# Storing the first slab in one piece and loading the projections in halves, in a kernel bound by its transfers

## The chip, the core and the metric

The kernel runs on one core of a Trainium2 chip. The core has five engines with queues of their own (TensorE or PE, VectorE or DVE, ScalarE or ACT, GpSimd or POOL, SyncE or SP) and 16 DMA engines that move data between the off-chip memory (HBM) and the on-chip memory. The metric is the time of one execution on the device in microseconds (us), as the median of several. Time from the profile is counted from the span's start, which is the first instruction of the program.

## What is computed

```python
def reference(x, conditioning, gamma_proj, beta_proj):
    gamma = conditioning @ gamma_proj
    beta = conditioning @ beta_proj
    return (x * (1 + gamma[:, None, :]) + beta[:, None, :]).astype(np.float32)
```

All is float32. `x` is 32 x 512 x 256 (batch, sequence, channels), 16.8 MB; the output has the same size. `conditioning` is 32 x 64, each projection 64 x 256. Every element of `x` is read once, multiplied by one plus its gamma, has its beta added, and is written once.

## The kernel before

The batch is cut into four slabs of eight batch entries. A slab is a tile of 128 partitions with 32 rows of 256 channels each: 32 KB a partition, 4 MB in all. All four slabs stay in on-chip memory at once (`xs0` to `xs3`), the results overwrite the inputs there, and no buffer is used again.

**Loads.** SP issues all loads of `x` in order at the start (L60): slab 0 in four parts of eight rows (8 KB a partition), then slabs 1, 2 and 3 whole (32 KB a partition). ACT issues three small loads at the start: the conditioning (L49) and then the two projections into the halves of one tile `gbproj` (L51, L52), each 64 rows of 1 KB.

**Gamma and beta.** A matrix product with a widened identity (L73) turns the conditioning round and repeats each batch entry 16 times, so that each of 128 partitions has its entry's conditioning; DVE copies that to `cond_T` (L75). For each slab one matrix product on PE (L80) with `gbproj` gives gamma and beta for the slab's 128 partitions in PSUM (`gb_p`), and ACT copies both to on-chip memory, with 1 added to gamma (L83, L86), as `gb_s`. The first L80 waits for both projections.

**The main loop.** For each slab there are two groups of 16 rows. DVE does the first 11 rows of a group with two instructions (L101: gamma plus one times x; L104: plus beta) and POOL the other five (L103, L105). POOL's two L103 of a slab come before its two L105 in the order as built; DVE keeps the written order. So slab 0's first eight rows need nothing from POOL.

**Stores.** ACT issues the stores (L109), each as soon as the group that holds its last row is done. `STORES` says which rows go together: slab 0 in parts that end at rows 2, 8 and 32, so 2, 6 and 24 rows, or 2, 6 and 24 KB a partition; slabs 1 to 3 whole. The first two parts are issued after the first group, the third after the second.

**What sets the order.** Each engine runs its own instructions in order. Loads of `x` go through SP's DMA queue (q1 in the profile); the small loads and all stores go through ACT's (q10). Both are served by the same 16 DMA engines. A transfer with 128 partitions is cut into 128 packets, one per partition row, eight per DMA engine, and each DMA engine also writes one 4-byte completion per transfer. Completions go round eight semaphores, so a transfer's issue can wait for an earlier transfer that used the same one. SP ends the program only after all transfers have landed (the waits on L136).

Of the kernel before, what the change touches and what calls it, by code (L numbers as in the profile page):

```python
# [2 lines left out]

# [5 lines left out]


@with_exitstack
def kernel(
    ctx: ExitStack,
    tc: tile.TileContext,
    x: bass.AP,
    conditioning: bass.AP,
    gamma_proj: bass.AP,
    beta_proj: bass.AP,
    out: bass.AP,  # L20
):
    nc = tc.nc
    f32 = mybir.dt.float32
    ALU = mybir.AluOpType

    batch, seq, dim = x.shape
    cond_dim = conditioning.shape[1]
    P = 128
    SLABS = 4
    BS = batch // SLABS  # L30
    REP = P // BS
    ROWS = BS * seq // P
    assert SLABS * BS == batch and REP * BS == P and ROWS * REP == seq

    x_v = x.flatten_outer_dims().rearrange("(s p r) d -> s p r d", s=SLABS, p=P)
    o_v = out.flatten_outer_dims().rearrange("(s p r) d -> s p r d", s=SLABS, p=P)

    LOADS = {0: [8, 8, 8, 8]}
    STORES = {0: (2, 8, 32), 1: (32,), 2: (32,), 3: (32,)}
    GROUP = 16  # L40
    ON_DVE = 11

    consts = ctx.enter_context(tc.tile_pool(name="consts", bufs=1))
    xpool = ctx.enter_context(tc.tile_pool(name="xpool", bufs=1))
    psum = ctx.enter_context(tc.tile_pool(name="psum", bufs=1, space=bass.MemoryType.PSUM))


    cond_s = consts.tile([batch, cond_dim], f32)
    nc.scalar.dma_start(out=cond_s, in_=conditioning)  # L49
    gbproj = consts.tile([cond_dim, 2 * dim], f32)  # L50
    nc.scalar.dma_start(out=gbproj[:, :dim], in_=gamma_proj)  # L51
    nc.scalar.dma_start(out=gbproj[:, dim:], in_=beta_proj)  # L52

    slabs = []
    for s in range(SLABS):
        xs = xpool.tile([P, ROWS, dim], f32, name=f"xs{s}")
        slabs.append(xs)
        r = 0
        for n in LOADS.get(s, [ROWS]):
            nc.sync.dma_start(out=xs[:, r : r + n, :], in_=x_v[s, :, r : r + n, :])  # L60
            r += n
        assert r == ROWS


    ident = consts.tile([batch, batch], f32)
    make_identity(nc, ident)
    rident = consts.tile([batch, batch * REP], f32)
    nc.vector.tensor_copy(  # L68
        out=rident.rearrange("p (b g) -> p b g", g=REP),
        in_=ident.to_broadcast([batch, batch, REP]),  # L70
    )
    cond_T_p = psum.tile([cond_dim, batch * REP], f32)
    nc.tensor.matmul(cond_T_p, lhsT=cond_s, rhs=rident, start=True, stop=True)  # L73
    cond_T = consts.tile([cond_dim, batch * REP], f32)
    nc.vector.tensor_copy(out=cond_T, in_=cond_T_p)  # L75

    gb_p, gb_s = [], []
    for s in range(SLABS):
        p_t = psum.tile([P, 2 * dim], f32, name=f"gb_p{s}")
        nc.tensor.matmul(p_t, lhsT=cond_T[:, s * P : (s + 1) * P], rhs=gbproj,  # L80
                         start=True, stop=True)
        s_t = consts.tile([P, 2 * dim], f32, name=f"gb_s{s}")
        nc.scalar.activation(out=s_t[:, :dim], in_=p_t[:, :dim],  # L83
                             func=mybir.ActivationFunctionType.Identity,
                             bias=1.0, scale=1.0)
        nc.scalar.copy(out=s_t[:, dim:], in_=p_t[:, dim:])  # L86
        gb_p.append(p_t)
        gb_s.append(s_t)

    def rows(t, n):  # L90
        return bass.AP(tensor=t.tensor, offset=t.offset, ap=[t.ap[0], [0, n], t.ap[1]])

    for s in range(SLABS):
        xs = slabs[s]
        g_p, b_p = gb_p[s][:, :dim], gb_p[s][:, dim:]
        g_s, b_s = gb_s[s][:, :dim], gb_s[s][:, dim:]
        for r0 in range(0, ROWS, GROUP):
            v = xs[:, r0 : r0 + ON_DVE, :]
            w = xs[:, r0 + ON_DVE : r0 + GROUP, :]
            nv, nw = ON_DVE, GROUP - ON_DVE  # L100
            nc.vector.scalar_tensor_tensor(out=v, in0=rows(g_p, nv), scalar=1.0, in1=v,  # L101
                                           op0=ALU.add, op1=ALU.mult)
            nc.gpsimd.tensor_tensor(out=w, in0=w, in1=rows(g_s, nw), op=ALU.mult)  # L103
            nc.vector.tensor_add(out=v, in0=v, in1=rows(b_p, nv))  # L104
            nc.gpsimd.tensor_tensor(out=w, in0=w, in1=rows(b_s, nw), op=ALU.add)  # L105

            for e0, e1 in zip((0,) + STORES[s], STORES[s]):
                if r0 < e1 <= r0 + GROUP:
                    nc.scalar.dma_start(out=o_v[s, :, e0:e1, :], in_=xs[:, e0:e1, :])  # L109
        assert STORES[s][-1] == ROWS  # L110


# [1 line left out]
_INS = ['x', 'conditioning', 'gamma_proj', 'beta_proj']  # L114
_OUTS = [((32, 512, 256), 'float32')]


# [23 lines left out]
```

## Time and profile before

| | |
|---|---|
| median of 3 runs | 84.33 us (84.33 to 84.34) |
| the profiled execution's own time | 84.33 us |
| its span, first to last instruction | 82.6 us |
| bytes moved | 33.69 MB, mean 408 GB/s |
| packets | 2080 |
| DVE busy | 49.9 us (60% of the span) |
| POOL busy | 46.3 us (56%) |
| PE busy | 9.1 us (11%) |
| ACT busy | 3.9 us (5%) |
| first instruction of the main loop on DVE | 12.10 us |
| last instruction on DVE, end | 61.18 us |

The profile page gives, for each engine, the busy time and a strip of 40 slices (about 2 us each) with the busy share in tenths; the strip named DMA is the mean busy share of the 16 DMA engines. The chain is followed back from the last instruction to what released each step. A group of instructions has the source line, the engine, the operation, and the mean duration of one. The list of DMA issues gives the size of each transfer and its time "to landing", from issue to the completion of its last packet. Asked for a window, the trace gives the packets that start in it for each queue, their bytes, and the time they took as a share of 16 engines over the window. Packets of different lines can be compared in this way: a window that holds one size of packet on one queue gives the duration of a single packet.

### The profile page before, as it was taken

To read this page: it belongs to the slowest core of one execution; us is meant where nothing else is said; L and a number is where in the kernel's file an instruction comes from. 1 tells how busy PE (TensorE), PEld (TensorE's weight loads), DVE (VectorE), ACT (ScalarE), POOL (GpSimd) and SP (SyncE) were. 2 spreads that over 40 slices of the span, in tenths; PEclk is the share of its full clock that TensorE was granted. 3 is DMA by queue.
4 is the path that set the end of the run, shared out by engine and by line. 5 is a ranking of instruction groups with operands and counts; after the bars stand their busy time and mean duration, and the time that the engine had idled before them with its cause. 6 is when DMAs were issued, how large, how long until landed. Compare 5 with 4: busy or idle time off the path is not lost.

```text
span 82.6 us, 154 instructions
## 1 busy us (share of the span) xinstructions
PE 9.1 (11%) x10; PEld 2.8 (3%) x10; DVE 49.9 (60%) x18; ACT 3.9 (5%) x9; POOL 46.3 (56%) x22
## 2 busy tenths in 40 slices
PE   0090499900000000000000000000000000000000
PEld 0010243100000000000000000000000000000000
DVE  2002019999999999999999999999960000000000
ACT  0600033330000000000000000000000000000000
POOL 2000029999999999999999999999000000000000
DMA  3899999799899796979997999998998998999890
GB/s 48 322 422 380 421 425 591 333 429 508 351 458 508 303 539 284 605 318 460 445 445 302 453 476 405 508 397 365 508 460 349 460 508 349 413 508 413 349 508 0
DMA packets 2080, 33.69 MB, mean 408 GB/s; under 512 B 288, under 2 KB 416, under 8 KB 672
## 3 DMA queue, kind: packets, MB, share of 16 engines
q1 hardware_dynamic: 1008, 16.78, 48.7%
q10 hardware_dynamic: 1072, 16.92, 47.8%
HBM read 16.92 MB, written 16.78 MB: 408 GB/s over the span
## 4 chain that ended last, share of the span: by engine, by line
DVE 48%; issue 12%; DMA 9%; PE 2%; ACTq 1%; ACT 1%
DVE xs L101 30%; DVE xs L104 19%; DMA gbproj<-in_beta_proj_dram 9%; PE gb_p L80 2%; ACTq L51 1%; ACTq L49 0%; ACT gb_s L83 0%; ACT gb_s L86 0%
## 5 line engine op out<-in xcount | busy, mean ns | idle before, releaser
L103 POOL TENSOR_TENSOR xs<-xs,gb_s 128x1280 f32<-128x1280 f32 x8 | 23.0, 2898 | 11.0 <-ACT gb_s L83 10.8
L101 DVE SCALAR_TENSOR_TENSOR xs<-gb_p,xs 128x2816 f32<-128x2816 f32 x8 | 24.7, 3085 | 5.3 <-ACT gb_s L86 5.3
L104 DVE TENSOR_TENSOR xs<-xs,gb_p 128x2816 f32<-128x2816 f32 x8 | 24.7, 3088 | 0.3
L105 POOL TENSOR_TENSOR xs<-xs,gb_s 128x1280 f32<-128x1280 f32 x8 | 23.0, 2893 | 0.0
L80 PE MATMUL gb_p<-gbproj,cond_T 64*128 64x512 f32 x8 | 7.2, 1074 | 3.3 <-DMA gbproj<-in_beta_proj_dram 3.3
L75 DVE COPY cond_T<-cond_T_p 64x512 f32<-64x512 f32 x1 | 0.7, 682 | 4.5 <-PE cond_T_p L73 4.5
L80 PEld LDWEIGHTS gb_p<-gbproj,cond_T 64*128 64x128 f32 x8 | 2.5, 326 | 8.1 <-issue 8.1
L73 PE MATMUL cond_T_p<-rident,cond_s 32*64 32x512 f32 x2 | 1.9, 1068 | 4.1 <-DMA cond_s<-in_conditioning_dram 4.1
L83 ACT ACTIVATE gb_s<-gb_p 128x256 f32<-128x256 f32 x4 | 1.5, 385 | 11.0 <-PE gb_p L80 11.0
L86 ACT COPY gb_s<-gb_p 128x256 f32<-128x256 f32 x4 | 1.5, 368 | 0.0
L83 ACT ACT_TABLE_LOAD x1 | 1.3, 1283 | 2.4 <-issue 2.4
L68 DVE COPY rident<-ident 32x512 f32<-32x512 f32 x1 | 0.4, 414 | 1.2 <-POOL ident masks.py:199 1.2
L73 PEld LDWEIGHTS cond_T_p<-rident,cond_s 32*64 32x64 f32 x2 | 0.3, 198 | 4.1 <-issue 4.1
masks.py:197 POOL MEMSET ident<- 32x32 f32 x1 | 0.1, 116 | 0.3 <-POOLq L125 0.3
masks.py:199 POOL TENSOR_SCALAR_AFFINE_SELECT ident<-ident 32x32 f32<-32x32 f32 x1 | 0.2, 205 | 0.1
L125 POOL MEMSET const-float32-0.0<- 128x1 f32 x1 | 0.1, 104 | 0.2 <-issue 0.2
L125 POOL MEMSET const-uint8-127<- 128x1 uint8 x1 | 0.1, 108 | 0.0
L125 POOL MEMSET const-bfloat16-1.0<- 128x1 bf16 x1 | 0.1, 106 | 0.0
L125 POOL MEMSET const-float32-1.0<- 128x1 f32 x1 | 0.1, 103 | 0.0
## 6 DMA issues: line engine op xcount, KB each, us to landing
xs<-in_x_dram SPq DMA_DIRECT2D x3, 4096.0 KB, 26.2
out_dram<-xs ACTq DMA_DIRECT2D x3, 4096.0 KB, 23.1
xs<-in_x_dram SPq DMA_DIRECT2D x4, 1024.0 KB, 8.5
out_dram<-xs ACTq DMA_DIRECT2D x1, 3072.0 KB, 28.2
out_dram<-xs ACTq DMA_DIRECT2D x1, 768.0 KB, 25.1
out_dram<-xs ACTq DMA_DIRECT2D x1, 256.0 KB, 14.0
gbproj<-in_gamma_proj_dram ACTq DMA_DIRECT2D x1, 64.0 KB, 6.4
gbproj<-in_beta_proj_dram ACTq DMA_DIRECT2D x1, 64.0 KB, 7.5
```

Of the source, the lines that this page charges most:

```text
L51: nc.scalar.dma_start(out=gbproj[:, :dim], in_=gamma_proj)
L68: nc.vector.tensor_copy(out=rident.rearrange("p (b g) -> p b g", g=REP), in_=ident.to_broadcast([batch, batch, REP]),)
L73: nc.tensor.matmul(cond_T_p, lhsT=cond_s, rhs=rident, start=True, stop=True)
L75: nc.vector.tensor_copy(out=cond_T, in_=cond_T_p)
L80: nc.tensor.matmul(p_t, lhsT=cond_T[:, s * P : (s + 1) * P], rhs=gbproj, start=True, stop=True)
L83: nc.scalar.activation(out=s_t[:, :dim], in_=p_t[:, :dim], func=mybir.ActivationFunctionType.Identity, bias=1.0, scale=1.0)
L86: nc.scalar.copy(out=s_t[:, dim:], in_=p_t[:, dim:])
L101: nc.vector.scalar_tensor_tensor(out=v, in0=rows(g_p, nv), scalar=1.0, in1=v, op0=ALU.add, op1=ALU.mult)
L103: nc.gpsimd.tensor_tensor(out=w, in0=w, in1=rows(g_s, nw), op=ALU.mult)
L104: nc.vector.tensor_add(out=v, in0=v, in1=rows(b_p, nv))
L105: nc.gpsimd.tensor_tensor(out=w, in0=w, in1=rows(b_s, nw), op=ALU.add)
L125: nc = _bacc.Bacc("TRN2", target_bir_lowering=False, num_devices=1)
```

## The change

Two edits. The store of slab 0 goes out whole, like those of the other slabs. Each projection is loaded by two DMAs of 32 rows each, in place of one of 64. The sizes and the order of the loads of `x`, the computation and its order on PE, DVE and POOL stay as they are. ACT issues five small loads in place of three and four stores in place of six; the numbers of lines after L52 go up by one.

```diff
-    STORES = {0: (2, 8, 32), 1: (32,), 2: (32,), 3: (32,)}
+    STORES = {0: (32,), 1: (32,), 2: (32,), 3: (32,)}
...
-    nc.scalar.dma_start(out=gbproj[:, :dim], in_=gamma_proj)
-    nc.scalar.dma_start(out=gbproj[:, dim:], in_=beta_proj)
+    for half, proj in ((gbproj[:, :dim], gamma_proj), (gbproj[:, dim:], beta_proj)):
+        for c0 in range(0, cond_dim, 32):
+            nc.scalar.dma_start(out=half[c0 : c0 + 32, :], in_=proj[c0 : c0 + 32, :])
```

## The prediction

> **What bounds the kernel now.** I read the page's row of DMA by slices first, then the chain of work, then the waits of the DMA queue's engine (SP), then the time to landing of single DMAs by narrow windows.
>
> From the page:
> ```profile
> span 82.6 us, 154 instructions
> DMA  3899999799899796979997999998998998999890
> ...
> DVE 48%; issue 12%; DMA 9%; PE 2%; ACTq 1%; ACT 1%
> ...
> xs<-in_x_dram SPq DMA_DIRECT2D x3, 4096.0 KB, 26.2
> out_dram<-xs ACTq DMA_DIRECT2D x3, 4096.0 KB, 23.1
> ```
> From the waits of SP:
> ```profile
> SPq L136 <- DMA out_dram<-xs: 47.7, 4, 18.8
> ```
> The DMA row is at eight or nine tenths in nearly every slice from 2 to 80 us. The chain names DVE, but it follows instructions back from DVE's last one, which the timeline ends at 61.2 us (58.09 + 3.09). The other 21 us are the stores still draining: SP's final waits are on the output. So the end is set by how long the 16 DMA engines need for all bytes, provided that they never run dry.
>
> The price of a transfer, from windows of the DMA view (first window 22.35 to 30.3 us, second 33 to 42, third 52.5 to 80; q1 carries the x loads, q10 the stores):
> ```profile
> q1 hardware_dynamic: 114, 3.21, 93.6%
> q10 hardware_dynamic: 115, 0.24, 7.6%
> ```
> ```profile
> DMA packets 230, 3.96 MB, mean 440 GB/s; under 512 B 15, under 2 KB 15, under 8 KB 131
> ...
> q1 hardware_dynamic: 114, 3.24, 83.5%
> q10 hardware_dynamic: 116, 0.71, 18.9%
> ```
> ```profile
> q10 hardware_dynamic: 394, 11.86, 99.9%
> ```
> The columns are packets, MB and share of 16 engines. Two readings. First, packets go one for one: 114 against 115, though a load packet is 32 KB and a store packet here 2 KB. An engine with work in both queues gives them **turns**, whatever the size. Second, the price: 0.076 x 7.95 us x 16 engines / 115 = 0.084 us for a 2 KB packet; 0.189 x 9 x 16 / 116 = 0.234 us for 6 KB; 0.999 x 27.5 x 16 / 362 (394 less 32 completions) = 1.213 us for 32 KB. The window 44.5 to 51.8 gives 0.912 us for 24 KB in the same way. A slab has 128 packets, 8 per engine: 9.70 us.
>
> So today the slab-0 store in thin rows hardly slows the loads, and pays for it in its own landing: the 256 KB part is issued at 18.35 and takes 14.0 us. The last x load lands at 46.3 (8.73 + 37.6), 2.5 us before DVE wants that slab:
> ```profile
> 45.84 3.09 DVE L104 TENSOR_TENSOR xs<-xs,gb_p 128x2816 f32<-128x2816 f32 x1
> ...
> 48.85 3.08 DVE L101 SCALAR_TENSOR_TENSOR xs<-gb_p,xs 128x2816 f32<-128x2816 f32 x1
> ```
>
> **The projections in halves (L51, L52).** ACT issues four DMAs of some 0.5 us in place of two (0.51 and 0.61). The same 128 rows of 1 KB move, but each engine gets two more completions, so two more turns behind 8 KB x packets. Gamma lands at 1.17 + 6.4 = 7.6, beta at 1.72 + 7.5 = 9.2: 1.6 us for beta's five turns (four rows and a completion), 0.32 each, so the last half lands 0.65 us later, at 9.86. L80, which waits for it (9.34), L83, L86 and the whole DVE chain (12.10) move with it. In the built order the eight completion semaphores shift round: the fourth slab-0 load now waits for cond_s (landed at 4.0), the slab-1 load for the first slab-0 part (5.6), slab 2 for gamma's first half and slab 3 for beta's first half. SP then issues slab 1 some 3 us later than at 2.86, but its packets' turn comes at 12.7, behind 4 MB, so that costs nothing. With fewer x issues ahead of them the halves may also land earlier. Bounds: 0.65 us sooner to 1.3 us later; I take +0.65. None of it reaches the end while the engines have x to load. In the engines' own time, the ten projection turns stand in a stretch where 8 KB packets run somewhat slow (about 0.2 us per engine altogether); two turns more are an estimate of +0.04, bounds -0.2 and +0.2.
>
> **The slab-0 store whole (L109).** Removed are two ACT issues and, per engine, 8 packets each of 2, 6 and 24 KB: 8 x (0.084 + 0.234 + 0.912) = 9.84 us. Added are 8 of 32 KB: 9.70. That is **-0.14 us**. Completions are equal (nine DMAs on this queue before and after).
>
> Two short stalls stand in the trace where one slab-0 part hands over to the next while loads run. In the windows 31.4 to 32.05 and 43 to 43.6, the sixteen load packets take:
> ```profile
> q1 hardware_dynamic: 16, 0.52, 194.8%
> ```
> ```profile
> q1 hardware_dynamic: 16, 0.52, 247.9%
> ```
> That is 1.948 x 0.65 = 1.27 us and 2.479 x 0.6 = 1.49 us a packet, 0.05 and 0.28 over 1.213. Two hand-overs become one (slab 0 to slab 1). If it costs as the first row, 0.28 goes; if the second row belongs to the last load packet of all, that recurs and only 0.05 goes. Bounds: -0.33, and +0.23 if the one left costs both rows' worse figure twice. I take the middle of the two readings, -0.17.
>
> **What moves: the loads of slabs 2 and 3.** The store is now issued after the whole slab, at 24.52 + 0.65 = 25.2. Today no q10 packet starts between 18.35 and 22.3, so a store finds its first turn 4.0 us after issue: 29.2, on the packet grid about 29.7. From 22.4 to there six of slab 2's eight packets have gone. The other two take turns with stores: with the completion's turn and 0.9 us to landing, slab 2 is there at 36.6, due at 36.60 + 0.65 = 37.25: no wait. Slab 3's eight then each pay a 32 KB store: 8 x 2.43, less one turn that slab 0's completion takes; they run to 55.2 and land at **56.1**. DVE wants them at 48.85 + 0.65 = 49.5: a new stall of 6.6 us. The slab takes 12.33 us (48.85 to 61.18), so it is done at 68.5, and its store is issued at 68.6, not 61.26.
>
> Does that show at the end? At 55.2 each engine has served 11 store packets (25.5 us / 2.43) and has 13 left of slabs 0 to 2: 13 x 1.213 = 15.8, to 70.9. Slab 3's packets must be ready by then. The first load shows issue to first packet on a free queue: 0.74 to about 1.75, 1.0 us. So 69.6, with **1.3 us to spare**. The DVE stall is hidden by the backlog, and if that cover goes, every microsecond counts in full.
>
> The Trainium skill ("DMA: Bandwidth & Descriptors", "Queues, rings and completion order") says that an engine drains a whole packet of typically 9 to 17 descriptors from one ring before it switches. This trace disagrees, with its 114 against 115. By that rule slab 0's eight would go in one piece, slab 3 would land near 52, and nothing could run dry; the sum would be the same.
>
> **Sum.** 84.33 - 0.14 - 0.17 + 0.04 = 84.06; I say 84.05. The profiled execution took 84.33 (span 82.6, 1.7 around it), the median of the three runs, so no correction is needed.
>
> **Rivals.** About 0.2% (0.17 us) is what a measurement here can tell from no change: below 84.16 is faster, over 84.50 slower.
> (A) As summed: the engines never run dry, 83.85 to 84.3. For it: the full DMA row. Chance 0.60, of it 0.42 faster, 0.18 same.
> (B) The engines run dry before the last store, which ends slower. The 4.0 us of the first store may be a latency of a loaded queue rather than its place behind packets already taken in; gamma, too, is issued at 1.17 and has its first packet only at 5.27. Then slab 3's packets come at 68.6 + 4.0 = 72.6 against 70.9: +1.7, in all 85.8. It decides from a latency of 2.3 us. Loads that come one packet later give up 1.2 us of the same margin, earlier projections likewise, so 84.5 to 85.8. Against it: 1.0 us on the free queue. Chance 0.28, of it 0.03 same.
> (C) Reads and writes of 32 KB in turn run slower than either alone. They alternate for 25.5 us, so each per cent is 0.26 us; at 2%, 84.6. Against it: 440 GB/s in the mixed window 33 to 42, no less than elsewhere. Chance 0.12, of it 0.03 same.
> Faster 0.42, same 0.24, slower 0.34. The range goes from A with both stalls gone (83.8) nearly to B's full price (85.6).
>
> **What would show it.** x landing to its maximum near 47 us (slab 3 issued near 9, landing at 56), a DVE wait of about 6.6 us before the seventh L101, DVE's end at 68.5, the last store landing about 13 us after its issue, the DMA row full to the end. A dip in the DMA row near slice 34 or 35 (70 to 72 us) is B. If slab 3 lands before 52, the turns are not as I read them; if more than 58, the engines will run dry and the prediction is wrong.

## The result, and the profile after

The changed kernel takes 84.69 us (median of six runs, 84.56 to 85.03) against 84.36 for the kernel before in the same comparison: a ratio of 1.0047, 95% interval 1.0025 to 1.0068. It is slower by about 0.33 us. Here and below, a median is of all runs, and a ratio is of the means of those runs that lie within 1.5% of the same kernel's fastest. The profiled execution took 84.56 (span 82.8), 0.23 more than the one of before.

The page of the changed kernel, the lines that answer to those shown of before, with the packet line and the queues:
```profile
span 82.8 us, 155 instructions
...
DMA  2799999899979989699799969969997996998890
...
DMA packets 1824, 33.69 MB, mean 407 GB/s; under 512 B 288, under 2 KB 416, under 8 KB 416
...
q1 hardware_dynamic: 1008, 16.78, 48.8%
q10 hardware_dynamic: 816, 16.92, 47.5%
...
DMA 67%; DVE 15%; ACTq 2%; issue 0%; DVEq 0%
...
out_dram<-xs ACTq DMA_DIRECT2D x4, 4096.0 KB, 22.6
xs<-in_x_dram SPq DMA_DIRECT2D x3, 4096.0 KB, 31.5
```
The DMA row is still full to the end. The chain now runs through transfers (67% DMA, 59% the loads of `x` alone), since DVE waits for the loads. The two queues of the kernel before:
```profile
q1 hardware_dynamic: 1008, 16.78, 48.7%
q10 hardware_dynamic: 1072, 16.92, 47.8%
```
Put the queues' shares on their spans: q10 took 0.475 x 82.8 = 39.3 us of 16 engines, before 0.478 x 82.6 = 39.5; q1 took 0.488 x 82.8 = 40.4, before 0.487 x 82.6 = 40.2. The stores got slightly cheaper and the unchanged loads dearer.

The timeline of DVE shows the new waits, before slab 2 (1.1 us) and before slab 3 (7.0 us), and the late last store:
```profile
25.23 45.42 ACTq L110 DMA_DIRECT2D out_dram<-xs  x4
...
38.52 3.09 DVE L102 SCALAR_TENSOR_TENSOR xs<-gb_p,xs 128x2816 f32<-128x2816 f32 x1 [1.11 <-DMA xs<-in_x_dram]
...
57.90 3.09 DVE L102 SCALAR_TENSOR_TENSOR xs<-gb_p,xs 128x2816 f32<-128x2816 f32 x1 [7.04 <-DMA xs<-in_x_dram]
```
The last store is issued at 70.3 us (the end of the first row's stretch, less its own 0.34) and lands 11.6 us later, at 81.95; before it landed at 81.72.

Where the loads got dearer is seen in narrow windows of the DMA view of the changed kernel, 27.5 to 28 us, 28.3 to 28.9 and 30.1 to 30.6, around the first packets of the whole slab-0 store (28.9 to 29.3 us on seven engines, 30.4 to 30.7 on nine):
```profile
q1 hardware_dynamic: 8, 0.26, 142.0%
```
```profile
q1 hardware_dynamic: 9, 0.29, 178.9%
```
```profile
q1 hardware_dynamic: 7, 0.23, 131.6%
q10 hardware_dynamic: 7, 0.23, 106.1%
```
A load packet takes 1.42 x 0.5 x 16 / 8 = 1.42 us in the first, 1.91 in the second and 1.50 in the third, not 1.213. Over all engines that is (8 x 0.21 + 9 x 0.70 + 7 x 0.29) / 16 = 0.62 us an engine. I call it the **stretch**. Before, it was 0.33 us in two places (31 and 43 us).

Once both kinds take turns, nothing is lost. The window 31.5 to 52 us of the changed kernel, 32 KB loads and 32 KB stores in turn (16 of each queue's packets are completions):
```profile
DMA packets 304, 8.91 MB, mean 435 GB/s; under 512 B 32, under 2 KB 32, under 8 KB 32
...
q1 hardware_dynamic: 153, 4.49, 50.7%
q10 hardware_dynamic: 151, 4.42, 50.0%
```
That is 0.507 x 20.5 x 16 / 137 = 1.21 us a load packet and 0.500 x 20.5 x 16 / 135 = 1.21 a store packet, as undisturbed.

### The profile page after: what moved, and what is told of

Same layout as the page of the kernel before. It is cut to its first block, busy times and chain, and to the rows that moved or that the text cites. A ratio compares the mean times of both kernels' runs of the same rounds, so it can differ in the third digit from the quotient of the medians.

```text
span 82.8 us, 155 instructions
## 1 busy us (share of the span) xinstructions
PE 9.1 (11%) x10; PEld 2.8 (3%) x10; DVE 50.1 (61%) x18; ACT 3.9 (5%) x9; POOL 46.3 (56%) x22
## 4 chain that ended last, share of the span: by engine, by line
DMA 67%; DVE 15%; ACTq 2%; issue 0%; DVEq 0%
DMA xs<-in_x_dram 59%; DMA gbproj<-in_beta_proj_dram 8%; DVE xs L105 7%; DVE xs L102 7%; ACTq L53 1%; ACTq L49 0%; DVEq L102 0%
## 6 DMA issues: line engine op xcount, KB each, us to landing
xs<-in_x_dram SPq DMA_DIRECT2D x3, 4096.0 KB, 31.5
```

## The experiments

After the result two theories stood. **Stretch**: the loss is that load packets are held up when the first large store packets come in. **Dry**: the engines run out of work before slab 3's late store. A third, that the split of the projections costs, was the rival to both. The runs of each experiment were taken beside runs of the kernel before on the same chip; the ratio is to those.

All stretches below are worked out as above from the packets' records (time over that of an undisturbed packet of the size, after 13 us, as a mean of 16 engines). The records name a packet's queue but not its engine. Where a single engine is spoken of, the packets were put in 16 lines by their times, each packet behind one that ends where it starts.

**1. The store whole, projections as before.**
```diff
-    STORES = {0: (2, 8, 32), 1: (32,), 2: (32,), 3: (32,)}
+    STORES = {0: (32,), 1: (32,), 2: (32,), 3: (32,)}
```


> The kernel before with one edit alone: slab 0 is stored whole; the projections are loaded as before. Theory 'stretch' (the loss is the stretching of load packets when the first 32 KB store packets come in, about 0.6 us an engine in place of 0.33, against 0.14 saved): about as the changed kernel's fastest runs, 84.5 to 84.6, in every run, and all four slab stores served without a gap. Theory 'dry' (the loss is that the engines run dry before slab 3's store): the main loop starts 0.7 us earlier, so the store of slab 0 takes turns with one load packet more, slab 3 lands up to 1.2 us later than 57.8, its store is issued near 71 or 71.5, and the engines idle 0.3 to 1.2 us near 71.5 us: 84.9 to 85.8. Theory 'projections' (the split is what costs): as before, 84.35.

Measured: 84.46 us, ratio 1.0031 (1.0004 to 1.0058). The runs lie in two groups, seven from 84.25 to 84.46 and four from 84.90 to 85.21. The profiled one (84.90) has a stretch of 0.44 us in the mean, which explains neither group. The window from 27 to 28 us shows the stretch, the one from 80.3 to 81 who was last:
```profile
q1 hardware_dynamic: 16, 0.52, 162.8%
```
```profile
q10 hardware_dynamic: 5, 0.03, 11.2%
```
Four completions and one 32 KB packet start after 80.3; the other 15 engines began their last packet earlier. That engine ended at 81.81, the next at 81.30. Followed back, its packets have two stretched loads, by 1.07 and 0.19 us, near 27 and 30 us, and no gap. Three engines did idle near 71.5, some 0.3 us in all, and ended earlier. So what counts is the stretch of the **unluckiest engine**; "dry" explains none of this profile's end.

**2. The split alone.**
```diff
-    nc.scalar.dma_start(out=gbproj[:, :dim], in_=gamma_proj)
-    nc.scalar.dma_start(out=gbproj[:, dim:], in_=beta_proj)
+    for half, proj in ((gbproj[:, :dim], gamma_proj), (gbproj[:, dim:], beta_proj)):
+        for c0 in range(0, cond_dim, 32):
+            nc.scalar.dma_start(out=half[c0 : c0 + 32, :], in_=proj[c0 : c0 + 32, :])
```


> The kernel before with the other edit alone: the projections are loaded in halves; slab 0 is stored in parts of 2, 6 and 24 rows as before. Theories 'stretch' and 'dry': 84.25 to 84.45, no difference from before, with the main loop 0.7 us later and stretched load packets of about 0.33 us an engine as before. Theory 'projections': 84.6 to 84.7.

Measured: 84.62, ratio 1.0045 (1.0020 to 1.0070). That refuted both theories as far as they left the split free. The engines tell little: stretch 0.32 as before, last landing 81.84 (61.95 + 19.9), 0.12 later. But from that landing to the span's end pass 1.05 us, before 0.83. The semaphore waits of SP from 81.5 us on, in the answer for the line of the program's end, of the kernel before, of the changed kernel and of this run:
```profile
L136 SPq EVENT_SEMAPHORE  x3: 17/17/28, 81.7 to 82.5; - x3
```
```profile
L137 SPq EVENT_SEMAPHORE  x3: 17/17/28, 82.0 to 82.7; - x3
```
```profile
L137 SPq EVENT_SEMAPHORE  x7: 17/28/36254, 45.6 to 82.8; - x7
```
Seven where there were three. The first of the seven had stood since 45.6, and held up those behind it until the last store landed. At the end SP waits for its semaphores, the eight of the completions among them, two at a time (a pair) and in a fixed order; a pair takes 0.06 us. Transfers take the eight semaphores in turn, so the number of transfers says which one the last store gets. With 16 it is on the last pair, with 18 on the second, and four pairs follow its landing. The changed kernel has 16 (two more small loads, two fewer stores), so it pays nothing; the split alone has 18.

**3. Slab 0's store behind the loads.** The changed kernel, with slab 0 stored by SP:
```diff
-                    nc.scalar.dma_start(out=o_v[s, :, e0:e1, :], in_=xs[:, e0:e1, :])
+                    eng = nc.sync if s == 0 else nc.scalar
+                    eng.dma_start(out=o_v[s, :, e0:e1, :], in_=xs[:, e0:e1, :])
```


> The changed kernel, but slab 0's whole store is issued by SP, so that it stands in the queue of the loads, behind them, and takes no turns from them. Both theories: slab 3 lands near 43 us, DVE does not wait for it, last DVE instruction ends near 62. 'Dry': no gap can open, so the whole loss goes; at most 84.2 to 84.3, all runs close together. 'Stretch': the first 32 KB store packets (slab 1's, near 40 us) still meet load packets; if they stretch them as in the changed kernel, 84.4 to 84.6, if none is stretched any more, 83.9 to 84.1.

Measured: 84.53, ratio 1.0017 (1.0003 to 1.0031). Slab 3 lands at 45.6, DVE waits for nothing, yet no gain against before. The stretch is 0.43 us, at 39 to 42 us, where the loads end and the first stores come. "Dry" is not the loss; "stretch" had 84.4 to 84.6 here.

**4. The last slab in halves**, so that no engine can wait for it. The changed kernel, with:
```diff
-    STORES = {0: (32,), 1: (32,), 2: (32,), 3: (32,)}
+    STORES = {0: (32,), 1: (32,), 2: (32,), 3: (16, 32)}
```


> The changed kernel, but the store of slab 3 goes out in halves of 16 rows, so its first packets are ready some 3 to 4 us earlier and cannot be late; nothing before 60 us differs. 'Stretch' alone: as the changed kernel's profiled run, 84.5 to 84.6, and the same spread from run to run as it (84.56 to 85.03). 'Dry' in part of the runs: 84.5 to 84.6 in every run, the slow ones of 84.96 and 85.03 are gone. 16 KB packets in place of 32 KB cost 8 x 0.01 us at most.

Measured: 84.84 (84.68 to 84.96), ratio 1.0053 (1.0035 to 1.0071). No engine idles, and it is no faster. It has 17 transfers and 0.99 us after the last landing, 0.16 more; without that it stands at 84.68, the changed kernel's median. Its stretch is 0.41 in the mean, and the engine with the most (0.29 and 0.62 in two packets) is the last by 0.37 us.

**5. All stores in the loads' queue.** The changed kernel, with:
```diff
-                    nc.scalar.dma_start(out=o_v[s, :, e0:e1, :], in_=xs[:, e0:e1, :])
+                    nc.sync.dma_start(out=o_v[s, :, e0:e1, :], in_=xs[:, e0:e1, :])
```


> The changed kernel, but all four slab stores are issued by SP, in the queue of the loads and behind them, so no store packet ever takes turns with a load packet. Transfers stay 16 in number, so the last store's completion is on the last pair that SP waits for, as in the kernel before and in the changed one (0.83 us from the last landing to the end). Theory 'stretch': no load packet after 13 us is stretched, and against the kernel before 0.33 us of stretching and 0.14 us of packet time are gone: 83.8 to 84.0, faster than both. If stretching is not tied to stores that meet loads: 84.3 to 84.6.

Measured: 84.40, ratio 0.9992 (0.9969 to 1.0016): no gain. Loads and stores never take turns here, yet the last loads before the first store are stretched by 0.22 us (window 40 to 41 us):
```profile
q1 hardware_dynamic: 14, 0.46, 127.2%
```
That is 1.272 x 16 / 14 = 1.45 us a packet. So a stretch needs no turns between loads and stores: it also stands where the last loads are followed by large stores in the same queue. My form of "stretch" was too narrow.

**6 and 7. The order of the final waits**, split and unsplit. Both have slab 0 loaded in two parts, the first on top of the split alone, the second on top of the kernel before:
```diff
-    LOADS = {0: [8, 8, 8, 8]}
+    LOADS = {0: [16, 16]}
```


> The split alone, as in the second run, but slab 0 is loaded in two parts of 16 rows in place of four of 8. That takes the transfers from 18 to 16, so that the last store's completion falls on the last pair of SP's final waits. The projections come some 3 us later, behind 16 KB packets, which the backlog hides. Theory 'order of the final waits': 0.83 us from the last landing to the end in place of 1.05, and 84.3 to 84.45, no slower than before. If the split costs in the engines or at the start: 84.55 to 84.7 again.

> The kernel before, with slab 0 loaded in two parts of 16 rows, the unsplit twin of the run above. The transfers go from 16 to 14, and the last store's completion falls on a pair with two more behind it. Theory 'order of the final waits': 0.95 us from the last landing to the end, 84.4 to 84.5: slower than the split twin by about 0.1, although it does less. If the split costs elsewhere: 84.3 or below and faster than the twin by 0.25.

Measured: 84.22 for the split one with 16 transfers, ratio 0.9978 (0.9965 to 0.9991), faster than before; 84.36 for the unsplit one with 14, ratio 0.9999 (0.9987 to 1.0010). The one that does more is faster by 0.14, and from last landing to end pass 0.83 and 0.95 us. The final waits are shown: 0.22 of the split's 0.28.

Neither was expected to be as fast as that. Their engines have a stretch of 0.00 and 0.04 us. The end of the loads in the split one, window 42.5 to 44.3 us:
```profile
DMA packets 62, 0.74 MB, mean 411 GB/s; under 512 B 11, under 2 KB 11, under 8 KB 46
...
q1 hardware_dynamic: 27, 0.52, 67.7%
```
27 less 11 completions are 16 load packets of 0.677 x 1.8 x 16 / 16 = 1.22 us. What it gains there it pays in part at the start, where its first slab-1 packets come 0.19 us later than before in the mean.

**8. The changed kernel again.**

> The changed kernel as it is, for a second profile and more runs. 'Stretch' alone: 84.5 to 84.7, load packets stretched by 0.4 to 0.6 us an engine, mean end of the engines' last packets 0.1 to 0.3 later than before, no engine idle near 71.5 us. 'Dry': runs over 84.9, and if the profiled one is among them, engines idle near 71.5 us by about the excess.

Measured: 84.64, ratio 1.0036 (1.0017 to 1.0056). This profile (84.79) has a stretch of 0.67 us, all but 0.02 of it from 27 to 31 us, in the window 27.4 to 30.6:
```profile
q1 hardware_dynamic: 26, 0.85, 78.2%
```
26 packets at 0.782 x 3.2 x 16 / 26 = 1.54 us. The engines' idle time is 0.06 us in the mean, all of it between 28.6 and 29.6 us, where the store comes in, and none near 71.5.

**9. Thin parts until the loads end.** The kernel before, with:
```diff
-    LOADS = {0: [8, 8, 8, 8]}
-    STORES = {0: (2, 8, 32), 1: (32,), 2: (32,), 3: (32,)}
+    LOADS = {0: [8, 8, 16]}
+    STORES = {0: (1, 2, 8, 32), 1: (32,), 2: (32,), 3: (32,)}
```


> The kernel before (projections not split), with slab 0 stored in parts of 1, 1, 6 and 24 rows and loaded in parts of 8, 8 and 16 rows, 16 transfers in all. Two thin parts of eight turns each last until the loads of x end near 44 us, so that no store packet over 1 KB meets a load packet. Theory 'stretch' (load packets are stretched when the first large store packets follow them in an engine): no stretching after 13 us, 0.33 us less than before, 0.03 more for smaller packets, 0.83 us from the last landing to the end: 84.0 to 84.15, faster than before by 0.2 to 0.35. If the gain of the sixth run came from its later main loop instead: 84.3 to 84.4.

Measured: 84.78 beside 84.50 for the kernel before on this chip, where that kernel's own runs spread from 84.34 to 85.59; ratio 1.0006 (0.9974 to 1.0039). The forecast missed: no run was below 84.48. The last load packets are stretched by 0.45 us (window 41 to 42):
```profile
q1 hardware_dynamic: 16, 0.52, 166.6%
q10 hardware_dynamic: 16, 0.01, 3.2%
```
Only 1 KB packets took turns with them, and 6 KB ones came next. So large store packets are not needed for a stretch at the loads' end.

**10. Parts of 8 and 24 rows.** The kernel before, with:
```diff
-    STORES = {0: (2, 8, 32), 1: (32,), 2: (32,), 3: (32,)}
+    STORES = {0: (8, 32), 1: (32,), 2: (32,), 3: (32,)}
```


> The kernel before, with slab 0 stored in parts of 8 and 24 rows: packets of 8 KB from 22.4 us and of 24 KB from about 35, both well inside the loads. 15 transfers: one more pair of waits behind the last store's completion, 0.06 us. Theory 'stretch': load packets are stretched by 0.1 to 0.3 us near 22 and by 0.3 to 0.6 near 34, so 0.4 to 0.9 in all against 0.33: 84.45 to 84.95. If a 24 KB packet among loads stretches nothing: 84.0 to 84.1 and the stretching belongs to the last load packet alone. No engine runs dry: slab 3 lands near 51 to 53.

Measured: 84.77 beside the same 84.50, ratio 1.0005 (0.9967 to 1.0043). The stretch has its forecast places: 0.05 us when the 8 KB packets come in (21 us; the forecast was 0.1 to 0.3), 0.44 when the 24 KB ones do (32 to 35; 0.3 to 0.6), and none at the loads' end (the last packet ends at 52.4). The entry of the 24 KB packets, window 33 to 34.6:
```profile
q1 hardware_dynamic: 16, 0.52, 100.3%
```
That is 1.003 x 1.6 x 16 / 16 = 1.60 us a load packet. The time does not separate this kernel from before.

**11. Slab 0 in four parts of 8 rows.** The kernel before, with:
```diff
-    LOADS = {0: [8, 8, 8, 8]}
-    STORES = {0: (2, 8, 32), 1: (32,), 2: (32,), 3: (32,)}
+    LOADS = {0: [8, 8, 16]}
+    STORES = {0: (8, 16, 24, 32), 1: (32,), 2: (32,), 3: (32,)}
```


> The kernel before (projections not split), with slab 0 stored in four parts of 8 rows, packets of 8 KB, and loaded in parts of 8, 8 and 16 rows, so 16 transfers. If the stretch belongs to the entry of store packets of 24 KB and more among load packets (0.41 to 0.67 us an engine in the five profiles that have it, 0 to 0.05 where the first store packets had 8 KB or less): 0 to 0.1 near 22 us, and with what the loads' end costs (0 to 0.45 in the profiles so far) 0 to 0.5 in all; slab 3 lands near 48. Best case 84.05 to 84.15, and 84.5 if the loads' end takes 0.45. If any 4 MB of stores among loads costs 0.4 to 0.7 whatever the packets: 84.5 to 84.8, with the stretching at 21 to 36 us.

Measured: 84.44, ratio 1.0014 (1.0004 to 1.0024). 0.05 us of stretch when the stores come in, 0.32 at the loads' end, window 45 to 46.5:
```profile
q1 hardware_dynamic: 16, 0.52, 102.5%
```
That is 1.025 x 1.5 x 16 / 16 = 1.54 us a load packet. The 4 MB among the loads do not cost by themselves; what costs at the entry goes with the size of the packets.

**12. The sixth again.**

> The kernel of the sixth run once more (projections split, slab 0 loaded in two parts and stored thin, 16 transfers), for a second profile and an interval from another set of runs. If its profile without any stretching is the rule, because its 24 KB packets come only after the last load packet: below the kernel before by 0.1 to 0.2 us again, stretch 0 to 0.05. If that was chance: as the kernel before or 0.1 above, stretch 0.2 to 0.45 near 42 to 44 us.

Measured: 84.07 (84.01 to 84.13), ratio 0.9966 (0.9953 to 0.9979), stretch 0.01. Again it is faster than the kernel before, by 0.3 us, and it lies 0.6 below the changed kernel's two medians (84.69 and 84.64).

**Together.** Two things go with most of the differences, the stretch and the waits behind the last landing:

| run | transfers | last landing to end, us | stretch, us an engine | where |
|---|---|---|---|---|
| before | 16 | 0.83 | 0.33 | loads' end 0.28 (24 KB stores follow), entry of 6 KB 0.05 |
| changed, and again (8) | 16 | 0.83 | 0.62, 0.67 | entry of 32 KB stores |
| 1 store alone | 14 | 0.95 | 0.44 | entry of 32 KB |
| 2 split alone | 18 | 1.05 | 0.32 | loads' end (24 KB follow) |
| 3 slab 0 behind loads | 16 | 0.83 | 0.43 | loads' end (32 KB follow) |
| 4 last slab in halves | 17 | 0.99 | 0.41 | entry of 32 KB |
| 5 all on SP | 16 | 0.83 | 0.22 | loads' end (32 KB follow) |
| 6, 12 | 16 | 0.83 | 0.00, 0.01 | - |
| 7 | 14 | 0.95 | 0.04 | loads' end |
| 9 | 16 | 0.83 | 0.45 | loads' end (6 KB follow) |
| 10 | 15 | 0.89 | 0.49 | entry of 24 KB 0.44, of 8 KB 0.05 |
| 11 | 16 | 0.83 | 0.38 | loads' end 0.32 (8 KB stores run on), entry of 8 KB 0.05 |

## Why the prediction was wrong

It forecast 84.05 and faster; measured were 84.69 and slower. That 84.69 lies in the stated range is luck: the upper part of the range was there for rivals B and C, and neither is what happened. Step by step:

- **The bound held.** The engines' work sets the end, and the kernels differ by tenths of a microsecond as that work, its disturbances and the waits after it do.
- **Packet time, -0.14: right.** The packets' plain durations sum to 78.36 us an engine in place of 78.50.
- **The split: right for this change, for an incomplete reason.** The last half landed at 9.92 (forecast 9.86) and DVE began at 12.82 (12.10 + 0.65 was 12.75). The first packets of slab 1 come 0.05 us later in the mean (forecast 0.04). What I did not see is that it adds two transfers, which alone costs 0.22 at the end (run 2); here the two stores removed take that back.
- **Turns: right in kind.** 127 load and 122 store packets start between 33 and 52 us in the changed kernel (143 and 138 with completions), 50.7% and 48.7% of the engines' time. The prediction's 114 also held 16 completions, so that only 98 were load packets; but in a window of before that holds none, 24 to 30.2 us, 75 load packets stand against 72 store packets, so the reading holds. What the Trainium skill ("DMA: Bandwidth & Descriptors", "Queues, rings and completion order") calls typical, 9 to 17 descriptors from one ring before a switch, is not seen here either, if a packet of the profile is one descriptor. Slab 3 landed at 57.8, forecast 56.1: on seven engines the store came in one load packet earlier than I had it, and the stretch held up the loads. DVE's wait was 7.0, forecast 6.6; its 1.1 us before slab 2 was forecast as none.
- **Rival B (dry), 0.28: not what happened, though close.** Of the 1.3 us to spare some 0.2 were left: the store is issued at 70.3, a microsecond to its first packet makes 71.3, and slab 2's store ends from 71.5 us on. (The prediction's 25.5 us hold 10.5 turns of 2.43, not 11; with that its own backlog would have ended at 71.6.) No engine idled there by more than 0.04 us. The idle time that the first profile has, 0.4 us over all engines or 0.03 in the mean, stands at 30.1 to 30.5 us, where the store comes in. Run 4, which can't run dry, is not faster.
- **Rival C (mixing), 0.12: refuted** by the window 31.5 to 52: 435 GB/s, 1.21 us a packet of either kind.
- **The step that failed: "Two hand-overs become one", -0.17.** Measured: +0.29 in the first profile (0.62 less 0.33), +0.34 in the second, outside even my bounds of -0.33 and +0.23. I took the two stalls of the kernel before for the price of a hand-over from one part of the store to the next, so that fewer parts would cost less. A hand-over as such costs next to nothing: from slab 0 to slab 1, near 49 us and in the middle of the loads, the changed kernel loses 0.00 us in the first profile and 0.02 in the second. It loses when the first 32 KB store packets come in among the loads, and for that entry the prediction had no term. Before, the packets that came in at 22.35 had 2 KB and cost nothing; those of the changed kernel are sixteen times the size.

The terms then are -0.14 + 0.29 + 0.05 = +0.20, for +0.23 in the profiled execution. The other 0.1 of the median is spread: in the second profile the stretch was larger and the last engine ended at 81.85, 0.39 after the mean.

**What stays open.** Why load packets stretch. Shown is where: at the entry of 24 or 32 KB stores with more loads to come (0.41 to 0.67 us in five profiles; 0 to 0.05 for 8 KB and less), or, in kernels without such an entry, at the loads' end (0.2 to 0.45 in six). In four of these six (before, runs 2, 3 and 5) the first 24 or 32 KB store packets come directly behind the stretched loads or one 6 KB packet later, so it may be the same effect; in runs 9 and 11 the packets that come next have 6 and 8 KB. Runs 6, 7 and 12 have next to none: there 6 KB packets, in service since 35 to 37 us, follow the last loads, and the 24 KB ones start at 44.5, behind them. Run 9, which meant to bring that about, had 0.45, and its 6 KB packets came in just at the loads' end. Neither the sizes nor the moment of entry were varied alone. That run 6 gains by the missing stretch is shown by its packets; that its later main loop causes it was not tried by itself.

## What to carry to other kernels

In a kernel bound by its transfers, look at the size of the packets in each queue. Here a DMA engine with two queues gave each a packet in turn, whether the store's packets had 2 or 32 KB, so the sizes decided how loads and stores shared the bandwidth; and load packets were held up when 24 or 32 KB store packets came in among them. Add up an edit's effect for the slowest engine rather than for the mean, since the last one ends the program. And when a change adds or removes transfers, look at the waits after the last landing before you look for a cause in the middle: here two edits that alone lengthened these waits by 0.12 and 0.22 us cancelled.

## What the runs showed that I had not expected

- The number of transfers, by itself, moves the end: 0.83 us from the last landing to the end with 16 transfers, 0.89 with 15, 0.95 with 14, 0.99 with 17 and 1.05 with 18.
- 32 KB loads and 32 KB stores in turn run at 435 GB/s and take 1.21 us a packet, as loads or stores alone.
- Load packets that take 1.213 us undisturbed took up to 2.28 us (run 1) when the first 32 KB store packets came in. In the changed kernel, loads and stores then took turns for 20 us without a loss.
